# A nanmax over rows with two of its three load buffers made wider, its key tiles regrouped and its last tiles divided anew

## The chip, the cores and the metric

The kernel runs on one core of a Trainium2 chip. The metric is the device time of one execution in microseconds. The profile is of one such execution; its span runs from the first to the last instruction of the program.

## The reference

The input is 32 x 2048 x 2048 float32, a tenth of it NaN. The result is the largest number of each row of 2048, NaN left out.

```python
x = np.random.randn(32, 2048, 2048).astype(np.float32)
x[np.random.rand(32, 2048, 2048) < 0.1] = np.nan

def reference(x, axis):            # axis = -1
    return np.nanmax(x, axis=axis).astype(np.float32)
```

That is 65536 rows, 512 for each of the 128 partitions, 537 MB to be read.

## The kernel before

**The unit** is a quarter row, 512 elements of 4 B in each partition (`Q`). A partition has 2048 of them. `TILES` divides them into 74 tiles; most are of 28 quarters (7 rows, 56 KB a partition, 7168 KB in all). An entry is (loads, pieces, reductions), each a list of numbers of quarters. `([28], [7, 9, 12], [16, 12])` is one load of 28, three pieces, and two reductions of 4 and 3 rows. Near the end the tiles are divided into more and smaller loads, pieces and reductions, down to single quarters.

**What is done to a piece.** SyncE (SP) loads it into one of three buffers `xt`. ScalarE (ACT) reads the upper 16 bits of each element and writes a "key" of 16 bits to a key tile `kt` (L222, `kt<-xt`); it maps NaN to a low number. Then GpSimd (POOL) maps the keys back into the upper halves of the elements (L232, `xt<-kt`), so that NaN has become very low. A piece with a minus sign is mapped back by ACT itself (L222, `xt<-kt`). A tuple of pieces shares one key instruction; a piece written as a float is mapped back after the next key instruction. VectorE (DVE) then takes the largest of each row (L239, `acc<-xt`).

**Order.** Each engine's instructions are issued in the order of the code; `Order.add` gives each the semaphore waits that its data need. A load into a buffer waits for the last reduction of the tile that was there three tiles earlier. The number of an entry counts from 1 where the code names tiles (`number` is raised before the loads are issued).

**Key tiles.** Before, there are three of 12 quarters. Pieces fill a key tile until one doesn't fit; then the next is taken, and the key instruction waits until the pieces that were there have been mapped back. The last piece of a tile of `TILES`, if it opens a key tile, waits for that one and for the one behind it:

```python
if used + c > KEYS:
    key = (key + 1) % NKEYS
    ...
    kold, kfree[key] = last(kfree[key]), []
    if at + c == sum(loads) * Q:
        kold = kold + last(kfree[(key + 1) % NKEYS])
```

**Joined events.** Where a reduction needs a piece of POOL and one of ACT, and nothing else needs them, `joints` gives both one semaphore, and one wait covers both. Both pieces count as mapped back only with that joined event, for the reduction and for the key tile (`cleaned`). Tiles whose number stands in `APART` have no such joints.

**Groups.** Consecutive tiles form six groups; a group's rows lie together in each partition, and its results are stored by one DMA of its own. A row of NaN alone is found by a last instruction on the results (`find`, L245, on VectorE for 414 rows and for the last 7; two on POOL for the 91 rows of group 4, L260 and L274).

Of the kernel before, what the change touches and what calls it, by code (L numbers as in the profile page):

```python
# [8 lines left out]
D = 2048  # L9

Q = D // 4
# [3 lines left out]

TILES = (
    [([4], [4], [4])]
    + [([28], [7, 9, 12], [16, 12])] * 7
    + [([28], [9, 12, -7], [8, 20])]
    + [([28], [7, 9, 12], [16, 12])] * 7  # L20
    + [([28], [9, 12, -7], [8, 20])]
    + [([28], [7, 9, 12], [16, 12])] * 7
    + [([28], [9, 12, -7], [8, 20])]
    + [([28], [7, 9, 12], [16, 12])] * 7
    + [([28], [9, 12, -7], [8, 20])]
    + [([28], [7, 9, 12], [16, 12])] * 7
    + [([28], [9, 12, -7], [8, 20])]
    + [([28], [7, 9, 12], [16, 12])] * 7
    + [([28], [6, 10, 12], [16, 12])] * 3
    + [([28], [7, 9, 12], [16, 12])]  # L30
    + [([28], [6, 10, 12], [16, 12])] * 3
    + [([28], [7, 9, 12], [12, 16])] * 2
    + [([28], [7, 10, 11], [12, 16])]
    + [([28], [6, 10, 12], [16, 12])] * 3
    + [([28], [8, 11, 9], [8, 8, 12])]
    + [([20, 8], [11, -6, 6, 5], [16, 12])]
    + [([20, 8], [12, (-4, 7), 5], [8, 8, 12])]
    + [([17, 11], [12, (-4, 6), 6], [4, 12, 12])]
    + [([16, 12], [11, -5, 5, 7], [16, 12])]
    + [([13, 15], [9, -4, 7, 8], [12, 8, 8])]  # L40
    + [([14, 14], [9, -4, 4, 4, 7], [12, 8, 8])]
    + [([11, 10, 7], [5, 6, (-3, 7), 7], [4, 4, 4, 8, 8])]
    + [([11, 9, 8], [4, 7, (-2, 7), 6, -2], [4, 4, 4, 8, 8])]
    + [([8, 7, 6, 7], [3, 5, 7, (3, -3), 3, 4], [8, 4, 8, 8])]
    + [([6, 5, 6, 5, 6], [5, (5, -1), (-1, 5), 5, 3, 3], [4, 4, 4, 4, 4, 4, 4])]
    + [([5, 6, 5, 4, 4, 3, 1], [(-2, 3), 3, 3, (4, -1), 4, 4, -2.0, 2], [4, 4, 3, 1, 4, 4, 4, 4])]
    + [([4, 4, 3, 2, 4, 2, 3, 3, 3], [2, 2, 4, (-2.0, 1), 2, 3, 3, (-1, 2), (1, -1, 1), 2, -1.0], [4, 4, 4, 4, 4, 4, 4])]
)

GROUPS = [TILES[i : i + 15] for i in range(0, 60, 15)] + [TILES[60:73], TILES[73:]]  # L50


FLAGGED = (3, 5)
LATE = 4

APART = (70, 71, 72, 73)
WIDE = 7
BUFS = 3

KEYS = 3 * D  # L60
NKEYS = 3

LEAD = 128

# [108 lines left out]
def kernel(  # L173
# [15 lines left out]
    nc = tc.nc  # L189
    P = nc.NUM_PARTITIONS  # L190
    f32, i32 = mybir.dt.float32, mybir.dt.int32
    i16, u16 = mybir.dt.int16, mybir.dt.uint16
    ALU = mybir.AluOpType
# [9 lines left out]
    rows = [sum(sum(loads) for loads, _, _ in g) * Q // D for g in GROUPS]  # L203
    assert R == P * sum(rows)

    sing = ctx.enter_context(tc.tile_pool(name="sing", bufs=1))

    scalars = sing.tile([P, LEAD // 4], f32, name="scalars")
    warm = scalars[:, 1:2]
    xts = [sing.tile([P, WIDE * D], i32, name=f"xt{i}") for i in range(BUFS)]  # L210
    kts = [sing.tile([P, KEYS], u16, name=f"kt{i}") for i in range(NKEYS)]
    accs = sing.tile([P, sum(rows)], f32, name="acc")
    late = sing.tile([P, rows[LATE]], i32, name="late")

    with tc.tile_critical():  # L215
        order = Order(nc)
# [24 lines left out]
        def find(deps, acc):  # L241
            return order.add(
                "dve",
                nc.vector,
                lambda: nc.vector.scalar_tensor_tensor(  # L245
                    out=acc,
                    in0=acc,
                    scalar=LEAST,
                    in1=acc,
                    op0=ALU.is_ge,  # L250
                    op1=ALU.mult,
                ),
                deps,
            )

        def find_late(deps, acc, none):
            e = order.add(
                "pool",
                nc.gpsimd,
                lambda: nc.gpsimd.tensor_scalar(  # L260
                    out=none,
                    in0=acc,
                    scalar1=LEAST,
                    scalar2=float(0x00400000),
                    op0=ALU.is_lt,
                    op1=ALU.mult,
                ),
                deps,
            )
            bits = acc.bitcast(i32)  # L270
            return order.add(
                "pool",
                nc.gpsimd,
                lambda: nc.gpsimd.tensor_tensor(out=bits, in0=bits, in1=none, op=ALU.add),  # L274
                [e],
            )

# [1 line left out]
        act([e_warm], out=warm, in_=warm, func=ACT.Prelu, alpha=0.5)  # L279

        free = [[] for _ in range(BUFS)]
        kfree = [[] for _ in range(NKEYS)]
        clock = 0

        def last(uses):

            return list({back: e for back, _, e in sorted(uses, key=lambda u: u[1])}.values())

        key = 0
        used = KEYS  # L290
        number = 0
        lanes = [[] for _ in range(LANES)]
        turn = 0
# [1 line left out]
        ready = []  # L295
        flagged = 0
        r0 = 0
        for gi, (s, g) in enumerate(zip(rows, GROUPS)):
# [1 line left out]
            og = of[r0 : r0 + P * s].rearrange("(p s) -> p s", p=P)  # L300
            r0 += P * s
            first = sum(rows[:gi])
            acc = accs[:, first : first + s]
            base = 0
            for loads, pieces, reds in g:
                assert sum(loads) == total(pieces) == sum(reds)
                xt, before = xts[number % BUFS], free[number % BUFS]
                number += 1
                landed = []
                at = 0  # L310
                for c in loads:
                    c *= Q
                    e = order.add(
                        "sp",
                        nc.sync,
                        lambda: nc.sync.dma_start(  # L316
                            out=xt[:, at : at + c], in_=xg[:, base + at : base + at + c]
                        ),
                        before + lanes[turn],
                        lane=f"load{turn}",  # L320
                        step=16,
# [6 lines left out]
                after = []  # L328
                at = done = 0
# [41 lines left out]
                for parts in pieces:  # L371
                    parts = parts if isinstance(parts, tuple) else (parts,)
                    c = int(sum(map(abs, parts))) * Q
                    here = [l for a, b, l in landed if a < at + c and b > at]
                    kold = []
                    if used + c > KEYS:
                        key = (key + 1) % NKEYS
                        used = 0
                        kold, kfree[key] = last(kfree[key]), []
                        assert all(k != key for q in half.values() for _, _, k, _, _ in q)  # L380
                        if at + c == sum(loads) * Q:

                            kold = kold + last(kfree[(key + 1) % NKEYS])
                    e_key = act(
                        here + kold,
                        out=kts[key][:, used : used + c],
# [7 lines left out]
                    for c in parts:  # L394
                        back, wait, c = c < 0, isinstance(c, float), int(abs(c)) * Q
# [8 lines left out]
                        else:  # L404
                            e = pool(
                                [e_key],
                                name(piece),
                                out=to,
                                in0=kp,
                                scalar1=-1.0,  # L410
                                scalar2=float(TOP),
                                op0=ALU.mult,
                                op1=ALU.add,
# [4 lines left out]
                        while reds and done + reds[0] <= min([at] + open_):  # L418
                            n = reds.pop(0)


                            lo = done - 1 if done % D else done
# [4 lines left out]
                            else:  # L427
                                m = max(n // D, 1)
                                to = acc[:, row : row + m]
                            e = dve(  # L430
                                [e for a, b, e in clean if b > lo and a < done] + part,
                                nc.vector.tensor_reduce,
                                out=to,
                                in_=xt[:, lo:done]
                                .bitcast(f32)
                                .rearrange("p (c d) -> p c d", c=m),
                                axis=mybir.AxisListType.X,
                                op=ALU.max,
                            )
                            part = [e] if done % D else []  # L440
                            after.append(e)
                free[(number - 1) % BUFS] = after[-1:]
                base += at
            stores.append((og, acc.bitcast(i32)))
            if gi == LATE:
                late_after = after
            elif gi not in FLAGGED:
                continue
            lo, flagged = flagged, first + s
            if gi == LATE:  # L450
                late_acc = accs[:, lo:flagged]
            else:
                e = find(after, accs[:, lo:flagged])
                ready += [e] * (gi + 1 - len(ready))
            if gi == len(GROUPS) - 1:
                ready[LATE] = find_late(late_after, late_acc, late)
        for (og, bits), e in zip(stores, ready):
            last = order.add(
                "sp",
                nc.sync,  # L460
                lambda: nc.sync.dma_start(out=og, in_=bits),
                [e],
                lane="store",
                step=16,
            )
# [38 lines left out]
```

## Time and profile before

| | |
|---|---|
| runs | 1252.53 us median of 3 (1252.44 to 1253.1) |
| the profiled execution | 1252.48 us, span 1250.7 us |
| VectorE busy | 1111.4 us (89%), 179 instructions |
| ScalarE busy | 965.6 us (77%), 273 instructions |
| GpSimd busy | 1168.5 us (93%), 242 instructions |
| DMA | 537.20 MB, mean 430 GB/s |

Busy shares are over the whole span; which engine ends last differs from stretch to stretch, and is read from the waits of that stretch. Times in the lines that follow are microseconds from the start of the span, and in the rows of groups "busy, mean ns of one | idle time before, and what ended it".

### The profile page before, as it was taken

The numbers are of one execution on the slowest core, as the hardware profiler recorded it, in microseconds if no ns is written. First come the engines' busy times: TensorE is split into PE (matmuls) and PEld (weight loads), VectorE is DVE, ScalarE is ACT, GpSimd is POOL, SyncE is SP. The second block draws the span as 40 slices with busy tenths as digits, with TensorE's granted clock in tenths as the row PEclk, the third lists the DMA queues.
The fourth block names the chain that finished last, engine by engine and source line by source line (L and its number), as shares of the span: only waits on it lengthen the run. The fifth ranks groups of instructions, "written<-read, shape, count | busy, mean of one in ns | idle before, by whom it ended". The sixth has DMA issues, their size and how long they took to land.

```text
span 1250.7 us, 891 instructions
## 1 busy us (share of the span) xinstructions
DVE 1111.4 (89%) x179; ACT 965.6 (77%) x273; POOL 1168.5 (93%) x242
## 2 busy tenths in 40 slices
DVE  0888989888889888898988888998888899999999
ACT  3777887778777877788777877777777778999997
POOL 2999989998999899998999899999999999989998
DMA  9999999999999999999999999999999999999997
GB/s 415 440 418 433 440 440 438 413 440 440 440 433 418 440 440 438 429 424 440 440 436 424 431 440 438 436 424 433 440 438 435 422 436 436 425 434 429 431 428 301
DMA packets 15991, 537.20 MB, mean 430 GB/s; under 512 B 2544, under 2 KB 2544, under 8 KB 3568
## 3 DMA queue, kind: packets, MB, share of 16 engines
q1 hardware_dynamic: 15984, 537.14, 99.4%
q14 instruction: 7, 0.06, 0.0%
HBM read 536.87 MB, written 0.26 MB: 429 GB/s over the span
## 4 chain that ended last, share of the span: by engine, by line
DMA 40%; DVE 29%; POOL 22%; ACT 9%; issue 1%; SPq 0%
DMA xt<-in_x_dram 40%; DVE acc L239 29%; POOL xt L232 22%; ACT kt L222 8%; ACT xt L222 1%; SPq L316 0%; DVE acc L245 0%; SPq L499 0%; SPq L215 0%
## 5 line engine op out<-in xcount | busy, mean ns | idle before, releaser
L232 POOL TENSOR_SCALAR xt<-kt 128x3584 int16<-128x3584 uint16 (+11 forms) x236 | 1167.4, 4947 | 77.6 <-ACT kt L222 63.9
L239 DVE TENSOR_REDUCE acc<-xt 128x3 f32<-128x6144 f32 (+4 forms) x175 | 1107.5, 6379 | 135.6 <-POOL xt L232 128.1
L222 ACT ACTIVATE kt<-xt 128x3584 uint16<-128x3584 int16 (+9 forms) x247 | 913.4, 3734 | 278.0 <-DMA xt<-in_x_dram 257.9
L222 ACT ACTIVATE xt<-kt 128x512 int16<-128x512 uint16 (+6 forms) x24 | 52.8, 2202 | 0.7
L245 DVE SCALAR_TENSOR_TENSOR acc<-acc 128x414 f32<-128x414 f32 (+1 forms) x2 | 2.2, 1111 | 0.1
L222 ACT ACT_TABLE_LOAD x1 | 1.3, 1283 | 0.9 <-SPq L215 0.9
L239 DVE TENSOR_REDUCE xt<-xt 128x1 f32<-128x1536 f32 x1 | 1.7, 1743 | 0.0
L278 DVE MEMSET scalars<- 128x1 f32 x1 | 0.1, 59 | 1.0 <-SPq L215 1.0
L260 POOL TENSOR_SCALAR late<-acc 128x91 int32<-128x91 f32 x1 | 0.5, 549 | 0.1
L274 POOL TENSOR_TENSOR acc<-acc,late 128x91 int32<-128x91 int32 x1 | 0.3, 341 | 0.1
L485 POOL MEMSET const-float32-0.0<- 128x1 f32 x1 | 0.1, 98 | 0.2 <-issue 0.2
L222 ACT ACTIVATE scalars<-scalars 128x1 f32<-128x1 f32 x1 | 0.2, 203 | 0.0
L485 POOL MEMSET const-bfloat16-1.0<- 128x1 bf16 x1 | 0.1, 101 | 0.0
L485 POOL MEMSET const-uint8-127<- 128x1 uint8 x1 | 0.1, 101 | 0.0
L485 POOL MEMSET const-float32-1.0<- 128x1 f32 x1 | 0.1, 98 | 0.0
## 6 DMA issues: line engine op xcount, KB each, us to landing
xt<-in_x_dram SPq DMA_DIRECT2D x61, 7168.0 KB, 22.6
xt<-in_x_dram SPq DMA_DIRECT2D x2, 5120.0 KB, 17.4
xt<-in_x_dram SPq DMA_DIRECT2D x3, 2816.0 KB, 22.7
xt<-in_x_dram SPq DMA_DIRECT2D x4, 2048.0 KB, 22.3
xt<-in_x_dram SPq DMA_DIRECT2D x5, 1536.0 KB, 29.1
xt<-in_x_dram SPq DMA_DIRECT2D x2, 3584.0 KB, 24.8
xt<-in_x_dram SPq DMA_DIRECT2D x6, 1024.0 KB, 26.8
xt<-in_x_dram SPq DMA_DIRECT2D x3, 1792.0 KB, 30.1
```

What stands on the lines that cost most here:

```text
L222: lambda: nc.scalar.activation(**kw),
L232: lambda: nc.gpsimd.tensor_scalar(**kw),
L239: return order.add("dve", nc.vector, lambda: do(**kw), deps)
L245: lambda: nc.vector.scalar_tensor_tensor(out=acc, in0=acc, scalar=LEAST, in1=acc, op0=ALU.is_ge, op1=ALU.mult,),
L260: lambda: nc.gpsimd.tensor_scalar(out=none, in0=acc, scalar1=LEAST, scalar2=float(0x00400000), op0=ALU.is_lt, op1=ALU.mult,),
L274: lambda: nc.gpsimd.tensor_tensor(out=bits, in0=bits, in1=none, op=ALU.add),
L278: e_warm = order.add("dve", nc.vector, lambda: nc.vector.memset(warm, 1.0), [])
L485: nc = _bacc.Bacc("TRN2", target_bir_lowering=False, num_devices=1)
```

## The change

- The three load buffers, the key tiles, and the results and flags of the last two groups lie in one tensor, `region`. For the first 43 tiles two of the three buffers have 32 quarters (64 KB a partition) and one has 28; tiles of 32, 32 and 28 take turns. There are then two key tiles of 11 quarters, and the last piece of a tile waits only for its own key tile.
- From tile 44 (`number == TURN` before it is raised) all three buffers have 28 quarters and there are three key tiles of 12, in the room that the wide buffers leave. The first pieces in each wait for what was in that room.
- `TILES` has 70 entries, six groups again (101, 107, 108, 98, 91 and 7 rows). Tiles 44 to 57 give ACT 7 quarters each to map back. From tile 58 on loads, pieces and reductions are divided anew. 2048 quarters as before; POOL maps back 1851 (before 1964), ACT 197 (before 84). Loads: 104 (before 105); reductions: 206 instructions (before 176).
- The flags of the first four groups (414 rows) are made by two instructions of VectorE with the flag in PSUM (`find_apart`), in place of one.

```diff
 TILES = (
     [([4], [4], [4])]
-    + [([28], [7, 9, 12], [16, 12])] * 7
+    + [([32], [10, 11, 11], [8, 12, 12])] * 2
+    + [([28], [8, 9, 11], [16, 12])]
+    + [([32], [10, 11, 11], [8, 12, 12])] * 2
+    + [([28], [8, 9, (6, -5)], [8, 8, 12])]
...
+    + [([28], [8, 9, 11], [12, 16])]
+    + [([32], [10, 11, 11], [8, 12, 12])]
+    + [([32], [10, (8, -3), 11], [8, 12, 12])]
+    + [([28], [(-3, 8), 11, -6.0], [8, 20])]
+    + [([28], [9, 12, -7.0], [8, 20])] * 7
+    + [([28], [10, 11, -7.0], [8, 20])]
     + [([28], [9, 12, -7], [8, 20])]
...
-    + [([28], [8, 11, 9], [8, 8, 12])]
-    + [([20, 8], [11, -6, 6, 5], [16, 12])]
-    + [([20, 8], [12, (-4, 7), 5], [8, 8, 12])]
-    + [([17, 11], [12, (-4, 6), 6], [4, 12, 12])]
-    + [([16, 12], [11, -5, 5, 7], [16, 12])]
-    + [([13, 15], [9, -4, 7, 8], [12, 8, 8])]
-    + [([14, 14], [9, -4, 4, 4, 7], [12, 8, 8])]
-    + [([11, 10, 7], [5, 6, (-3, 7), 7], [4, 4, 4, 8, 8])]
-    + [([11, 9, 8], [4, 7, (-2, 7), 6, -2], [4, 4, 4, 8, 8])]
...
+    + [([28], [9, 12, -7.0], [8, 20])] * 2
+    + [([28], [9, 12, -7], [8, 20])] * 3
+    + [([28], [8, 10, (5, -5.0)], [8, 4, 16])]
+    + [([28], [2, 6, 9, (8, -3)], [8, 8, 12])]
+    + [([18, 10], [8, 10, (6, -4.0)], [8, 8, 12])]
+    + [([18, 10], [8, 10, (7, -3.0)], [8, 8, 12])]
+    + [([18, 10], [8, 10, (6, -4.0)], [8, 8, 12])]
+    + [([16, 12], [8, 8, (-5, 7)], [8, 8, 12])]
+    + [([16, 12], [2, 3, 4, 7, 7, -5], [8, 8, 12])]
+    + [([14, 6, 8], [3, 4, (5, -1.0), 7, (-3, 5)], [4, 8, 8, 8])]
+    + [([11, 8, 9], [4, 7, (-3, 5), 5, 4], [4, 4, 4, 4, 8, 4])]
+    + [([8, 9, 6, 5], [(5, -3), 4, 4, (4, -3.0), (4, -1.0)], [8, 4, 4, 4, 8])]
+    + [([8, 5, 6, 5, 4], [2, 3, 3, 5, (3, 3), (-2, 3), (2, -2)], [4, 4, 4, 4, 4, 4, 4])]
+    + [([7, 5, 5, 4, 3, 4], [1, 3, 3, (-1, 4), (3, -2.0), 4, 3, (-1, 3)], [4, 4, 4, 3, 1, 4, 4, 4])]
+    + [([4, 4, 2, 1, 2, 4, 1, 1, 3, 1, 2, 1, 1, 1], [-1.0, 3, 2, (2, -2.0), 3, 1, 2, 3, -1.0, 2, (1, -1.0), 1, 2, -1], [4, 2, 2, 4, 4, 4, 4, 4])]
 )
-GROUPS = [TILES[i : i + 15] for i in range(0, 60, 15)] + [TILES[60:73], TILES[73:]]
+GROUPS = [TILES[i : i + 14] for i in range(0, 56, 14)] + [TILES[56:69], TILES[69:]]
-APART = (70, 71, 72, 73)
-WIDE = 7
+APART = (66, 67, 68, 69)
+WIDE = 32, 32, 28
+TAPER = 28
+TURN = 43
-KEYS = 3 * D
-NKEYS = 3
+KEYS = 11 * Q, 12 * Q
+NKEYS = 2, 3
...
-        def find_late(deps, acc, none):
+        def find_apart(who, engine, deps, acc, none, op):
             e = order.add(
-                "pool",
-                nc.gpsimd,
-                lambda: nc.gpsimd.tensor_scalar(
+                who,
+                engine,
+                lambda: engine.tensor_scalar(
                     out=none,
...
+                if number == TURN:
+                    a, b = kfree
+                    x0, x1 = ([("tile", 0, e) for e in free[i]] for i in range(2))
+                    assert slot == 0 and x0 and x1
+                    kts, kfree, stage = many, [a + x0, a + b, b + x1], 1
+                    key, used = NKEYS[1] - 1, KEYS[1]
+                xt, before = (lean if stage else wide)[slot], free[slot]
...
-                        if at + c == sum(loads) * Q:
-                            kold = kold + last(kfree[(key + 1) % NKEYS])
+                        if stage and at + c == sum(loads) * Q:
+                            kold = kold + last(kfree[(key + 1) % len(kts)])
```

## The prediction

> **What bounds the kernel now.** First the page's parts 1 to 3:
>
> ```profile
> span 1250.7 us, 891 instructions
> ...
> DVE 1111.4 (89%) x179; ACT 965.6 (77%) x273; POOL 1168.5 (93%) x242
> ...
> DMA packets 15991, 537.20 MB, mean 430 GB/s; under 512 B 2544, under 2 KB 2544, under 8 KB 3568
> ...
> q1 hardware_dynamic: 15984, 537.14, 99.4%
> ```
>
> The load queue is busy all through, so for most of the span the loads set the pace, and VectorE (DVE) and GpSimd (POOL) have to keep up. The 15984 packets are 105 loads of 128 data and 16 semaphore packets each, and 6 stores likewise: a load is one packet for each partition. Next the timeline of ScalarE (ACT), for the period of the loads:
>
> ```profile
> 73.38 7.12 ACT L222 ACTIVATE kt<-xt 128x3584 uint16<-128x3584 int16 x2 [4.10 <-DMA xt<-in_x_dram]
> 80.89 5.32 ACT L222 ACTIVATE kt<-xt 128x6144 uint16<-128x6144 int16 x1 [0.38 <-POOL xt L232]
> 90.27 7.12 ACT L222 ACTIVATE kt<-xt 128x3584 uint16<-128x3584 int16 x2 [4.06 <-DMA xt<-in_x_dram]
> ```
>
> A tile of 28 quarter rows lands every 90.27 - 73.38 = 16.89 us, 0.603 us a quarter. The packet records agree: 8 packets of 57344 B in turn on each of 16 engines, 2.114 us each, are 16.91.
>
> Then the timeline of VectorE near the end:
>
> ```profile
> 1034.56 23.79 DVE L239 TENSOR_REDUCE acc<-xt 128x4 f32<-128x8192 f32 x4
> 1058.51 162.84 DVE L239 TENSOR_REDUCE acc<-xt 128x3 f32<-128x6144 f32 x40 [0.16 <-POOL xt L232]
> ...
> 1223.04 24.87 DVE L239 TENSOR_REDUCE acc<-xt 128x1 f32<-128x513 f32 x12
> 1247.94 0.17 DVE L245 SCALAR_TENSOR_TENSOR acc<-acc 128x7 f32<-128x7 f32 x1
> ```
>
> From 1058.51 VectorE works without a pause to 1248.11. So the last 190 us have another bound: what ends last is VectorE's backlog, and any gap that a change opens there comes out at the end. From 1248.11 to the span's end are 2.59 us (the last store).
>
> Last the chain that ended last, for landings:
>
> ```profile
> 236.83 22.90 DMA xt<-in_x_dram
> ...
> 338.50 22.55 DMA xt<-in_x_dram
> ...
> 389.17 23.08 DMA xt<-in_x_dram
> ...
> 1110.46 20.76 DMA xt<-in_x_dram
> ```
>
> At 1110.46 + 20.76 = 1131.22 the first 1866 of 2048 quarter rows have landed. Pieces like 338.50 are the rule; those of 22.90 and 23.08 are stretched by 0.35 and 0.53 us.
>
> Durations, from the groups by form:
>
> ```profile
> L232 POOL TENSOR_SCALAR xt<-kt 128x3584 int16<-128x3584 uint16 x55 | 230.7, 4194 | 44.5 <-ACT kt L222 43.1
> ...
> L239 DVE TENSOR_REDUCE acc<-xt 128x2 f32<-128x4096 f32 x20 | 87.6, 4409 | 0.0
> L239 DVE TENSOR_REDUCE acc<-xt 128x1 f32<-128x2048 f32 x29 | 64.2, 2276 | 9.1 <-POOL xt L232 9.1
> ...
> L232 POOL TENSOR_SCALAR xt<-kt 128x2560 int16<-128x2560 uint16 x9 | 27.4, 3049 | 2.1 <-ACT kt L222 1.6
> ...
> L222 ACT ACTIVATE kt<-xt 128x4096 uint16<-128x4096 int16 x2 | 7.2, 3609 | 4.5 <-DMA xt<-in_x_dram 4.5
> ```
>
> Other forms are named with their means below. Hand-overs, from the same trace: landing to ACT 0.02 us, ACT to POOL 0.08, POOL to ACT or DVE 0.03; two POOL instructions in a row 0.08 apart; two independent ones of ACT or DVE overlap by 0.09 and 0.08.
>
> **The loads.** The bytes are the same; 105 loads become 104, and 28 of them carry 64 KB a partition. What does a load cost beyond its bytes? Eight times two packets of 28672 B (1.062 us) less eight of 57344 B (2.114), plus the semaphore packet (9 ns): 0.09 us; the landings (16384 B and 40960 B apart against together) say 0.05. The Trainium skill, in "DMA: Bandwidth & Descriptors", section "Anatomy of one DMA", gives another price: some 2.0 us fixed for each DMA beside the bytes, for a path that starts on GpSimd. These loads start on SyncE and are queued; here the row decides, since 7.34 MB land every 16.89 us. A 64 KB packet does not occur in the trace. By the rows of 2 KB to 56 KB (36.7 ns for 1000 B) it takes 2.415 us, a load of 32 quarters 19.3. The bound below: its share of fixed cost saved, already in the count of loads. The bound above: it is cut into two, 8 x 9 ns = 0.07 us a load, 28 x 0.07 = 2.0 us. I take the first, as all nineteen sizes of load packet in the trace lie on one line. The Trainium skill, same page, section "Why a DMA increments its semaphore by 16 and not by 1", speaks of rows longer than 64 KiB as those that have to be divided; by it exactly 64 KiB goes whole, and no run yet shows it.
>
> **Is the queue still fed in the wide tiles?** A tile of 32 that lands at T: ACT's 5120 form 4.46, POOL 5.91 + 6.48 + 6.48 with gaps, to T + 23.6, the last reduce of 12 quarters 6.54, so its buffer is free at T + 30.2. The next two loads land at T + 36.2 (16.9 + 19.3). SyncE issues 6.0 us before the queue would run dry; before, T = 73.36 is freed at 101.48, 5.7 ahead. The first load shows that a load into an empty queue needs 4.7 us to land, 2.5 of them packets, so 2.2 must remain: 3.8 are spare. Two key tiles of 11 hold ACT back until POOL is one piece behind, 4.9 us of ACT beside 6.5 of POOL: hidden, by 1.6 us. POOL has 19.1 of 19.3 us in a wide tile and 16.8 of 16.9 in [8, 9, 11]; every sixth tile gives ACT 5 quarters and lets POOL catch up. Without that cover a late POOL would first use up the 3.8 us.
>
> **Tiles 44 to 58** ([9, 12, -7] and kin): ACT 4.03 + 5.32 + 3.19 + 4.20 less overlaps, 16.6 of 16.9; the buffer is free at T + 4.1 + 5.34 + 3.2 + 4.2 + 10.8 = T + 27.7 of 33.8. Fed too. POOL loses 113 quarters of clearing (1964 to 1851), about 65 us, and ACT gains as much; neither ends last there, so this counts nothing.
>
> **Flags.** The 414-row flag of 2.06 us becomes two VectorE instructions through PSUM. Such a pair is not in the trace; from 0.3 (twice the 7-row flag's 0.17) to 4.1 (twice 2.06), nearest to the 0.55 + 0.34 of the 91-row pair on POOL. It stands at tile 56, where VectorE waits 1.6 us in every tile for ACT's 7 quarters, so I count nothing; were it 4.1, the idle time of tile 65 (next) would take up what remains.
>
> **The end, where I see the loss.** Number 65 is ([14, 6, 8], [3, 4, (5, -1.0), 7, (-3, 5)]). Its last key piece, of 8, opens a new key tile and by the code waits for that tile and the next one, which holds (5, -1). ACT's -1 and POOL's 7 are joined into one event (one reduce needs both), and a joined event frees both key tiles together. So the last piece waits until POOL has done the 7, and then POOL has nothing to do while ACT works. The price, step by step:
>
> - Number 65's first load completes 1894 quarters: 1131.22 + 28 x 0.603 + 0.05 (one load more) = 1148.16, less 5 loads that the new division has saved by then, 0 to 0.09 each, 0.05 taken: 1147.91.
> - ACT 1536 form 1.47, to 1149.40; POOL then runs 3, 4, 5, 7: 1.91 + 2.48 + 3.05 + 4.19 with gaps, to 1161.34.
> - ACT's piece of 8: 3.61, to 1164.98. POOL idle 3.7 us. POOL's 5: to 1168.11. VectorE, which reduces the 7's two rows from 1161.4 (or a little later) and is done by 1165.9, waits 2.2 and reduces 2 rows until 1172.55.
> - ACT after the 8: back 1.92, key of 4 1.90, key of 7 3.19, to 1171.8; POOL's 7 of number 66 to 1176.07. VectorE has reduced one row by 1174.8 and waits 1.4 more.
> - From 1176.1 VectorE has 34 rows left: 3 instructions of two rows (4.41 - 0.08) 13.0; 26 of one row (2.28 - 0.08) 57.0; two rows in two parts (1.74 and 0.69; two of 1.21 by the same line) 4.7. Together 74.7, to 1250.8. ACT and POOL stay ahead of it (least at 1181, by 0.05 us).
> - Flag 0.17, last store 2.59: a span of 1253.6, which is 2.9 over the 1250.7 of before.
>
> The profiled run's time was 1252.48 for a span of 1250.7, 1.78 around it, and it stands 0.05 under the median of 1252.53. So I forecast 1253.6 + 1.78 = **1255.4**, 0.23% slower. About 0.2% (2.5 us) is what a measurement of this kernel can tell from no change: slower begins at 1255.04, faster at 1250.02.
>
> **Rivals.**
> 1. *Not slower: the landings up to number 65 come earlier.* Everything behind that landing moves with it. The stretched pieces of the chain (0.35 and 0.53) and a third landing, 17.23 behind the one before it instead of 16.89, at 953, add 1.2 us; the runs of before spread over 0.66. If they are accidents of a run and not of the bytes, up to 1.2 falls away: 1254.2. It decides from 0.4 us on. For it: they fall on no special tile. Against: none of the three runs of before was without its share by more than 0.1 us. No change, 0.26, between 1253.8 and 1255.0.
> 2. *The change does not do what it says: a 64 KB packet is cut or slower.* 2.0 us on the stream, all of it ahead of number 65: 1257.4. Against it the straight line of the sizes; for it that the largest size seen is 56 KB. 0.14.
> 3. *Faster: a load has a real fixed cost.* Five loads fewer by number 65; to end below 1250.0 each must cost (5.4 + 0.25) / 5 = 1.1 us, where rows give 0.05 to 0.09. 0.06. By the skill's 2.0 us each it would be 1255.4 - 10 + 0.25 = 1245.7.
>
> The forecast itself keeps 0.50, from 1255.0 to 1256.3; 0.02 each remain for faster and for no change by what I don't see.
>
> **Range and chances.** Slower 0.50 + 0.14 = 0.64; no change 0.28; faster 0.08. The range takes in the forecast, the cut packets and rival 1 with some of its own error: 1252.8 to 1257.9.
>
> **What would show it.** Right: packets fall to 104 x 144 + 864 = 15840 on q1; VectorE waits for POOL near 1168 (2.2 us) and 1176 (1.4 us), and never after that; ACT's 4096 form starts near 1161.4, just as POOL ends a 3584; the end comes 8 to 9 us behind the last landing, near 1242. Cut packets would show as 19424 on q1. Wrong: VectorE without a gap from 1060 on, or a gap of SyncE's queue in the first 43 tiles.

## The result and the profile after

The changed kernel takes 1255.7 us (median of 10, 1255.57 to 1256.19); the kernel before, beside it, 1252.55 (median of 10). The ratio is 1.0025, with a 95% interval of 1.0015 to 1.0035: slower by 3.15 us. The profiled execution took 1255.72 for a span of 1253.9.

Of the page after, the lines that answer to the first ones shown of before:

```profile
span 1253.9 us, 966 instructions
...
DVE 1114.3 (89%) x210; ACT 1029.7 (82%) x286; POOL 1100.8 (88%) x226
...
DMA packets 15848, 537.21 MB, mean 428 GB/s; under 512 B 2528, under 2 KB 2528, under 8 KB 4064
...
q1 hardware_dynamic: 15840, 537.14, 99.1%
q14 instruction: 8, 0.07, 0.0%
```

Queue q1 moved 15840 packets, 144 for each of 104 loads and six stores: a load of 64 KB a partition is still one packet for each partition. POOL is busy 67.7 us less and ACT 64.1 us more, and the time has not followed either.

The timeline of ScalarE (ACT) early on, for the period of the loads (start, duration, engine, line, operation, forms, and in brackets the idle time before):

```profile
80.72 9.26 ACT L279 ACTIVATE region<-region 128x5120 uint16<-128x5120 int16 x2 [2.94 <-DMA region<-in_x_dram]
91.21 4.90 ACT L279 ACTIVATE region<-region 128x5632 uint16<-128x5632 int16 x1 [1.23 <-POOL region L289]
100.01 9.26 ACT L279 ACTIVATE region<-region 128x5120 uint16<-128x5120 int16 x2 [3.91 <-DMA region<-in_x_dram]
```

A wide tile lands 100.01 - 80.72 = 19.29 us after the one before it, 0.603 us a quarter, as before with 28. The wide loads have not changed the pace.

The timeline of VectorE (DVE) near the end:

```profile
1098.98 67.10 DVE L296 TENSOR_REDUCE region<-region 128x2 f32<-128x4096 f32 x14
1168.35 6.61 DVE L296 TENSOR_REDUCE region<-region 128x2 f32<-128x4096 f32 x2 [2.27 <-POOL region L289]
1176.28 74.86 DVE L296 TENSOR_REDUCE region<-region 128x1 f32<-128x2048 f32 x33 [1.32 <-POOL region L289]
1251.18 0.17 DVE L302 SCALAR_TENSOR_TENSOR region<-region 128x7 f32<-128x7 f32 x1
```

Here is the loss: two gaps, 2.27 and 1.32 us, in a stretch in which the kernel before had 0.16. Behind the second one VectorE works without a pause to 1251.14, so nothing is caught up. The span is 3.2 us longer. With 84 rows left VectorE stands at 1064.18, where the kernel before stood at 1065.07: it is 0.89 us ahead. It loses 3.59 in the two gaps, and the work on these 84 rows, in 56 instructions where there were 52, takes 0.53 longer: 3.59 - 0.89 + 0.53 = 3.23.

Where the gaps come from, in the timelines of ACT and of POOL for the same window:

```profile
1139.64 18.16 ACT L279 ACTIVATE region<-region 128x3584 uint16<-128x3584 int16 x8
1161.58 25.29 ACT L279 ACTIVATE region<-region 128x4096 uint16<-128x4096 int16 x10 [3.78 <-POOL region L289]
```

```profile
1149.68 11.86 POOL L289 TENSOR_SCALAR region<-region 128x1536 int16<-128x1536 uint16 x4 [1.52 <-ACT region L279]
1165.28 3.04 POOL L289 TENSOR_SCALAR region<-region 128x2560 int16<-128x2560 uint16 x1 [3.73 <-ACT region L279]
```

ACT stands 3.78 us for POOL before the key instruction of 8 quarters of number 65; POOL, which finishes its fourth piece at 1161.54, then stands 3.73 us for that very instruction. Two engines that should overlap take turns once, and VectorE runs out of rows behind them.

### The profile page after: what moved, and what is told of

The parts are those of the page before. It is cut to its first block, busy times and chain, and to the rows that moved or that the text cites. A ratio compares the mean times of both kernels' runs of the same rounds, so it can differ in the third digit from the quotient of the medians.

```text
span 1253.9 us, 966 instructions
## 1 busy us (share of the span) xinstructions
DVE 1114.3 (89%) x210; ACT 1029.7 (82%) x286; POOL 1100.8 (88%) x226
## 3 DMA queue, kind: packets, MB, share of 16 engines
q1 hardware_dynamic: 15840, 537.14, 99.1%
## 4 chain that ended last, share of the span: by engine, by line
DMA 33%; POOL 24%; ACT 21%; DVE 21%; issue 1%; SPq 0%; ACTq 0%
DMA region<-in_x_dram 33%; POOL region L289 24%; ACT region L279 21%; DVE acc L296 15%; DVE region L296 6%; SPq L380 0%; ACTq L178 0%; DVE region L302 0%; SPq L567 0%; SPq L272 0%
## 5 line engine op out<-in xcount | busy, mean ns | idle before, releaser
L289 POOL TENSOR_SCALAR region<-region 128x5632 int16<-128x5632 uint16 (+9 forms) x220 | 1099.7, 4999 | 146.3 <-ACT region L279 133.6
L279 ACT ACTIVATE region<-region 128x5632 uint16<-128x5632 int16 (+15 forms) x284 | 1028.2, 3668 | 215.3 <-POOL region L289 113.5
L296 DVE TENSOR_REDUCE acc<-region 128x3 f32<-128x6144 f32 (+4 forms) x145 | 899.4, 6240 | 131.7 <-POOL region L289 109.4
L296 DVE TENSOR_REDUCE region<-region 128x1 f32<-128x2048 f32 (+8 forms) x61 | 213.5, 3571 | 4.3 <-POOL region L289 3.6
```

The source lines that it names most:

```text
L279: lambda: nc.scalar.activation(**kw),
L289: lambda: nc.gpsimd.tensor_scalar(**kw),
L296: return order.add("dve", nc.vector, lambda: do(**kw), deps)
```

## The experiments

Every run is timed in five rounds against the kernel before on the same chip; its time stands beside that kernel's. That is 1252.73 us for the joint and the look-ahead taken away, the front without wide loads and the old front with the new end as it is; 1252.8 for the last run, the smaller stall; and 1252.56 for the other four.

**The joint taken away.** The pieces of number 65 that are joined get events of their own again. By the code of `joints` there are two such pairs: the -1 with the 7, which the forecast is about, and the -3 with the 5 in the last piece.

```diff
-APART = (66, 67, 68, 69)
+APART = (65, 66, 67, 68, 69)
```

> The changed kernel with number 65 added to APART: its pieces of POOL and ACT keep events of their own, so the key tile that holds (5, -1) is free once ACT has mapped the 1 back, and the last key piece of 8 starts when its data land (near 1156.6) instead of 1161.6. Nothing else differs; results are the same. Theory (the joined event at number 65 makes the loss): POOL's idle 3.7 us before its piece of 5 and VectorE's waits of 2.27 and 1.32 us go, VectorE runs without a pause from about 1055 on, and the time falls by 2.8 to 3.5 us to 1252.0 to 1252.8. Rival A (the wide loads and the new room cost the time): 1255.7 stays, only the waits' place moves. Rival B (more and smaller loads and reductions at the end cost the time): 1255 to 1255.7.

1252.83 us, ratio 1.0001 (0.9992 to 1.001). Of the 3.15 us all but 0.10 are gone with one number; the time lies at the upper edge of what was expected. POOL's timeline:

```profile
1149.79 15.02 POOL L289 TENSOR_SCALAR region<-region 128x1536 int16<-128x1536 uint16 x5 [1.47 <-ACT region L279]
1165.34 2.48 POOL L289 TENSOR_SCALAR region<-region 128x2048 int16<-128x2048 uint16 x1 [0.53 <-ACT region L279]
```

The five pieces of number 65 now follow one another; where POOL stood 3.73 us there is no gap. VectorE's timeline:

```profile
1038.37 167.09 DVE L296 TENSOR_REDUCE region<-region 128x5 f32<-128x10240 f32 x39 [0.37 <-ACT region L279]
1205.91 42.30 DVE L296 TENSOR_REDUCE region<-region 128x1 f32<-128x2048 f32 x21 [0.45 <-POOL region L289]
```

Behind 1060 one wait is left that was not expected, 0.45 us at 1205.46. Rivals A and B, that wide loads or the finer end cost the time, both fall with this run.

**The look-ahead taken away.** The joint stays; the last piece of number 65 waits only for its own key tile.

```diff
-                        if stage and at + c == sum(loads) * Q:
+                        if stage and number != 65 and at + c == sum(loads) * Q:
```

> The changed kernel where the last piece of number 65 alone waits only for its own key tile, not for the next one too; the joined event stays. Theory: both are needed for the stall, so this undoes it as fully as taking the joint away: 1252.0 to 1252.8, POOL's 3.7 us gone. If the joined event by itself held something up (its reduction, or the key tile's reuse one piece later), some of the 3 us would stay: 1253.5 to 1255.7. Rivals A and B as before: no change from 1255.7.

1252.87 us, ratio 1.0001 (0.9993 to 1.001), as with the joint taken away and 0.07 above the range expected. VectorE's waits from 1030 to the end (us in total, times, longest):

```profile
DVE acc L296 <- ACT region L279: 1.6, 1, 1.6
DVE region L296 <- ACT region L279: 0.4, 1, 0.4
```

None of them is for POOL. The joint alone does no harm. The stall needs both: an event that comes late, and a wait that asks for a key tile which the piece does not yet use.

**Joints at 66 to 69 put back**, 65 alone apart:

```diff
-APART = (66, 67, 68, 69)
+APART = (65,)
```

> The changed kernel with APART holding 65 alone, so that numbers 66 to 69 are joined. Control: joints as such cost nothing, only the one before a last piece with nothing left to do for POOL. Theory: as with 65 to 69 apart, 1252.6 to 1253.1. If any joint near the end costs, up to 1255.7.

1252.76 us, ratio 1.0002 (0.9993 to 1.001). By the code of `joints` number 66 has nothing to join; 67, 68 and 69 have five pairs. These cost nothing that the comparison can tell, though VectorE sets the end there.

**The front without wide loads.**

```diff
-    + [([32], [10, 11, 11], [8, 12, 12])] * 2
-    + [([28], [8, 9, 11], [16, 12])]
...
+    + ([([28], [8, 9, 11], [16, 12])] * 2 + [([28], [8, 9, (6, -5)], [8, 8, 12])]) * 15
...
-TURN = 43
+TURN = 46
```

> The changed kernel with no load over 28 quarters: the first 1264 quarters in 46 tiles of 4 and 28 (pieces [8, 9, 11], every third [8, 9, (6, -5)]) in the same buffers, two key tiles of 11 as before, and everything from the tile (-3, 8), 11, -6 on unchanged (numbers moved by 4; the three key tiles come one tile earlier). Theory: the front hardly counts while the queue is fed; 4 loads more at 0.05 us each: 1255.6 to 1256.1, with VectorE's two waits as in the changed kernel. Rival A (64 KB loads cost time): 1253 to 1254. The opposite (64 KB loads gain time that the end hides): 1257 and more.

1255.97 us, ratio 1.0026 (1.0016 to 1.0036): the time of the changed kernel, with VectorE's waits (3.2 us for POOL in two behind 1060). Against the kernel before on its own chip it is 3.24 us slower, the changed kernel 3.15. The 28 wide loads, and the four loads that they save, are together worth 0.1 us, within the noise of the comparison.

**The old front with the new end.** The last 12 tiles (from quarter 1712) of the changed kernel in the kernel before, first as they are:

> The kernel before with its last 12 tiles (from quarter 1712 on) replaced by the last 12 of the changed kernel; buffers, key tiles, flags and everything ahead are those of before. The joint then stands at number 69. Theory: the whole loss comes with these 12 tiles: 1255.6 to 1256.4, with VectorE waiting for POOL twice, about 1.5 and 1.4 us, near 1169 and 1177. Rival A (wide loads, new room): as fast as before, 1252.3 to 1253.0.

1256.27 us, ratio 1.0028 (1.0017 to 1.0039). VectorE's timeline shows the two gaps, the first of them smaller, in a kernel that has neither wide buffers nor `region`:

```profile
1168.99 6.61 DVE L239 TENSOR_REDUCE acc<-xt 128x2 f32<-128x4096 f32 x2 [1.43 <-POOL xt L232]
1176.92 11.00 DVE L239 TENSOR_REDUCE acc<-xt 128x1 f32<-128x2048 f32 x4 [1.31 <-POOL xt L232]
```

Then with that tile, there number 69, apart:

```diff
-APART = (70, 71, 72, 73)
+APART = (69, 70, 71, 72, 73)
```

> The kernel before with the last 12 tiles of the changed kernel, as before, and number 69 (the one with the joint) added to APART. Theory: the loss goes as it did on the new front: from 1256.27 down by 2.9 to 3.4, 1252.9 to 1253.4, with no wait of VectorE over 0.3 us behind 1060. If the new end had a cost of its own beside the joint, it would stay above that: 1254 and more.

1253.18 us, ratio 1.0005 (0.9996 to 1.0014). Over the kernel before on the same chips that is 3.54 with the joint and 0.62 without: the joint costs 2.9 us here, and 3.15 - 0.10 = 3.05 on the new front. The 0.6 that is left here was not followed up.

**The new front with the old end.** The other way round, the last 12 tiles of before behind the new front.

> The changed kernel with its last 12 tiles replaced by the last 12 of the kernel before (the same APART numbers, 66 to 69). Theory: an end pays for each wait of VectorE behind 1060, and this end meets the new front out of step: waits of about 1.1, 0.6 and 1.2 us near 1065, 1075 and 1082, so 1254.0 to 1254.7, between the two. If the new end alone were the cause and the front no matter, 1252.3 to 1253.0.

1254.46 us, ratio 1.0015 (1.0006 to 1.0023). ACT and POOL do not take turns here, as ACT works without a pause from 1046.62 to 1096.89. And yet:

```profile
1065.51 8.69 DVE L296 TENSOR_REDUCE region<-region 128x4 f32<-128x8192 f32 x1 [1.09 <-POOL region L289]
1074.72 6.55 DVE L296 TENSOR_REDUCE region<-region 128x3 f32<-128x6144 f32 x1 [0.53 <-POOL region L289]
1082.46 30.32 DVE L296 TENSOR_REDUCE region<-region 128x2 f32<-128x4096 f32 x6 [1.18 <-POOL region L289]
```

Three gaps of VectorE's timeline, 2.8 us in all, and a time 1.9 over the kernel before; why not the full 2.8 was not followed up. POOL, for which VectorE waits, itself waited 3.31 and 2.46 us for ACT in this stretch, so ACT was behind. An end is as good as its fit to the tiles ahead of it: neither the new front nor the old end loses this by itself.

**A stall in the front.** On the kernel without the joint, number 10 gets a stall of the same kind.

```diff
+                        if number == 10 and at + c == sum(loads) * Q:
+                            kold = kold + [e_pool]
...
+                            e_pool = e
                             cleaned(at - c, at, key, piece, e)
```

> The kernel with number 65 unjoined (1252.83), and one stall of the same kind put into the front: the last key piece (11 quarters) of number 10 waits also for POOL's piece of 9 just ahead of it, so POOL has nothing to do for the 4.9 us of that key instruction. Theory (there the load queue's reserve of 3.8 us covers what POOL loses, and the rest is paid once): 0.6 to 1.2 us, 1253.4 to 1254.0, with the queue empty once, near 227. If a stall counts in full wherever it is: 4.9, 1257.7. If the front covers all of it: 1252.8.

1255.01 us, ratio 1.0021 (1.0012 to 1.003): a miss. The stall is there, as large as planned (POOL's timeline):

```profile
194.50 6.46 POOL L289 TENSOR_SCALAR region<-region 128x5632 int16<-128x5632 uint16 x1 [5.01 <-ACT region L279]
```

Over the unjoined kernel it cost 2.35 us (2.45 against 0.10, each over the kernel before on its own chip), not 0.6 to 1.2, though less than half of its 5.0. The trace shows where it arose. A load issued at 207.58, 3.6 us before the landing ahead of it at 211.19 (its lead is 3.6 us), landed 17.50 behind that, not 16.89. The next was issued at 226.67, 2.0 us ahead, and landed 21.08 behind, not 19.29. Its first packet started at 227.64, just as the load ahead ended on the first of the 16 engines, so the queue did not run dry; but its first packets took 2.42 to 3.27 us where 2.418 is the rule. A third, issued at 245.77, 4.0 us ahead, landed 19.83 behind. The profiled run was the slowest of the eleven (1255.97): its landing of 1894 quarters is 3.1 us behind that of the unjoined kernel (1151.23 against 1148.14), and its span is 3.2 longer. The reserve that the prediction gave to the load queue was too large.

**A smaller one**, to tell how large the reserve is: number 10 divided so that POOL stands for a key of 6.

```diff
-    + [([28], [8, 9, 11], [16, 12])]
+    + [([28], [11, 11, 6], [8, 12, 8])]
```

> As the run with a stall in the front, with number 10 divided into [11, 11, 6], so that POOL stands for the 2.8 us of a key of 6 instead of 4.9. Loads are then issued at the least 2.8 to 3.0 us before the load ahead has landed (undisturbed 5.9, with the larger stall 1.3 to 2.4). Theory 1, as the prediction had it (2.2 us ahead are enough): no cost, 1252.6 to 1253.0. Theory 2 (a load issued less than some 4 us ahead starts late or slowly on the 16 engines, as the trace with the larger stall suggests: 207.58 issued, 211.19 the landing ahead, yet the next landing 0.6 late): 0.4 to 1.2, 1253.2 to 1254.0.

1254.17 us, ratio 1.0009 (1.0 to 1.0018). That is 1.27 us over the unjoined kernel (1.37 against 0.10), a little more than theory 2 allowed. The runs spread from 1252.83 to 1255.19; those of the kernel before, on the same chip, from 1252.55 to 1253.37, and the unjoined kernel's, on another, stayed within 0.4. In the profiled run the load of 225.79, issued 2.9 us ahead of the landing at 228.69, landed 20.48 behind it, 1.2 late. So a lead of some 3 us is already too little, and theory 1 falls. Theory 2 is right that a late issue costs before the queue runs dry, but its "some 4 us" is no clean limit: in the run without wide loads five loads issued 3.95 to 4.44 us ahead landed on time (16.89 to 16.93 behind).

None of these beats the kernel before by more than the comparison can tell; the unjoined kernel equals it.

## Why the prediction was right

**The end, step by step.** Each term of the sum against the trace of the changed kernel:

| step | forecast | trace |
|---|---|---|
| landing of 1894 quarters | 1147.91 | 1148.04 |
| POOL done with the piece of 7 | 1161.34 | 1161.54 |
| POOL idle behind it | 3.7 | 3.73 |
| VectorE's waits | 2.2 and 1.4 | 2.27 and 1.32 |
| last stretch of VectorE | 1176.1, 74.7 long | 1176.28, 74.86 long |
| span | 1253.6 | 1253.9 |
| time | 1255.4 | 1255.7 (median) |

The step that carried it was to read two bounds from the profile, not one: the loads up to some 1058, VectorE's backlog behind that. The code alone shows a wait; that it is paid is in VectorE's row, which had no idle time left there. The joint's gaps (3.59 us, less the 0.45 that the unjoined kernel has) came out as 3.05 us of time. One thing held by little: no wait behind 1176 was forecast with a margin of 0.05 us at 1181, and in the unjoined kernel one of 0.45 us does come.

**The loads.** A packet of 64 KB took 2.418 us, against 2.415 from the line of the other sizes, and none was cut. On the limit the Trainium skill ("DMA: Bandwidth & Descriptors", section "Why a DMA increments its semaphore by 16 and not by 1") speaks only of rows longer than 64 KiB as divided, and the trace agrees: a row of exactly 64 KiB went in one piece. Its fixed cost of some 2.0 us for each DMA (section "Anatomy of one DMA", for the path that starts on GpSimd) does not show in this fed queue: four loads more, in the run without wide loads, cost 0.1 us together. Only the runs with a stall, where the queue was nearly empty, have landings that are late by that order, 1.2 and 1.8 us; that this is the same cost is not shown, as it was packets that took longer there.

**The queue's reserve was mis-sized.** The buffer times were right: the load that waits for the tile landed at 80.64 was issued at 110.89, T + 30.25 (forecast 30.2), 5.95 us ahead of the landing at 116.84 (forecast 6.0). But "2.2 must remain: 3.8 are spare" took the start of the first load as the price of a late one. The two stalls show losses at leads of 2.0, 2.9 and 3.6, and 5.95 is harmless, so the spare is less than 5.95 - 3.61 = 2.3. In the front of the changed kernel the shortest lead is 4.63, and none of its loads lands over 0.1 us late but the three in which instruction packets run (next paragraph), so the forecast did not suffer.

**Rival 1 rested on an error.** It took the stretched landings for possible accidents of a run. They belong to the program. The packet records have them where a packet of 8192 B of queue q14, the instruction queue, runs: before, at 248.2, 254.5, 385.6, 939.9 and 999.0; after, at 270.2, 276.5, 311.8 and 806.6; in the unjoined kernel at 272.4, 276.7, 312.0 and 806.7. Each takes 0.31 us, and as it ends a load packet starts that takes 0.22 to 0.53 us longer than the rule before, 0.22 to 0.54 after. Runs of kernels with the same front have these packets at the same places, within 2.5 us. The landings that they fall in are late by 1.2 us in sum before, by 1.15 after and by 0.9 in the unjoined kernel, against 16.88 us for 28 quarters and 19.29 for 32. So the versions pay about the same, and the chance of "no change" was set too high for this reason.

**Rivals 2 and 3** fall with the 15840 packets and with the run without wide loads.

**What counted nothing.** The flags took 0.59 + 0.59 us, within the bounds and below the 2.06 of before; POOL's 67.7 us less moved nothing, as the loads set the pace in the front both before and after.

## What to carry to other kernels

Ask for each stretch which engine has no idle time left; a gap opened there is paid almost in full (3.05 us for 3.14 here), and one in another stretch only in part (2.35 us for 5.0 in the front). Where one event stands for the work of two engines, and a wait asks for a resource ahead of its use, look for the place where both meet: that is where two engines begin to take turns. The reserve of a queue is measured by making the issue late; the latency of the first transfer gave it too large here.

## What the runs showed of the hardware that was not expected

- A load that is issued late slows the stream before the queue runs dry: leads of 3.6, 2.9 and 2.0 us ahead of the landing before it cost 0.6, 1.2 and 1.8 us on that landing, in packets that took up to 3.27 us in place of 2.418. With the smaller stall the time then scattered by 2.4 us from run to run (1252.83 to 1255.19), where the kernel before on the same chip stayed within 0.8. The lead alone does not decide it: with 4.0 us one load behind a stall was 0.5 us late, and five in the run without wide loads, with 3.95 to 4.44 us, were on time. Where between 3.6 us and the 5.9 of the undisturbed stream the loss begins, and on what else it depends, stays open.
- Packets of the instruction queue hold up the loads. In the kernel before a load packet ended at 385.60, a packet of 8192 B of q14 ran from 385.60 to 385.91, and the next load packet started at 385.90 and took 2.647 us, not 2.116. So one engine loses 0.5 to 0.85 us to such a packet (0.31 for itself, 0.22 to 0.54 for the one behind it), and the load lands with the last engine. The records do not name the engine; that it is the same one is read from the times. It was not tried to take these packets away.
